# Exp in place in PSUM, low halves of the probabilities on VectorE, and scaling and rotation of latent queries and keys on GpSimd, in a two-layer hybrid encoder

## The chip, the core and the metric

The kernel runs on one core of one Trainium2 chip. Its engines are TensorE (PE in the profile: matmul, with weight loads listed apart as PEld), VectorE (DVE), ScalarE (ACT), GpSimd (POOL) and SyncE (SP, which issues the transfers here). They run side by side, each through its own queue in order, and wait for one another by semaphores. The metric is the device time of one execution in microseconds. Before the change it is 1695.26 us, the median of three runs that lie between 1694.22 and 1695.61 us.

## What is computed

Two layers over 512 tokens with 1024 channels, all in float32. Each layer has an attention part with three branches and a gated MLP with a convolution of width three:

```python
proj = rms_norm(x) @ w_in          # latent q, latent kv, rotary key, GQA q/k/v, pool, gates
# branch A, latent attention: 8 heads, 64 plain + 32 rotary dimensions
q = rms_norm((rms_norm(c_q) @ w_uq).reshape(b, s, 8, 96), qh_g)
k = rms_norm(concat(k_nope, broadcast(k_rope_raw)), kh_g)
q, k = rope on the last 32 of 96
# branch B, grouped-query attention: 8 heads of 64, 2 key/value heads, normed and rotated
# branch C: centred mean pooling minus token, with a linear map
# both attentions: softmax(q k^T / sqrt(d)) v
merged = sum(sigmoid(gate_i) * (o_i @ w_branch_i))
x = x + merged @ w_out
x = x + (silu(conv(h @ w_up)[gate]) * conv(h @ w_up)[val]) @ w_down
```

The normalisation of q and k is a multiplication by the inverse square root of a mean square, per token and head.

## The kernel before

Everything is kept with 128 partitions. Activations of the trunk lie channel by token (`XM`, eight tiles of 128 x 512); queries and keys are made token by channel, because their norm is per token, and are turned by TensorE into channel by token.

**Two halves.** TensorE multiplies in a reduced float32 format. So each operand is split: the high half is the value rounded to that format, the low half is the value minus the high half. A product is three matmuls: high by high, high by low, low by high (`mm3`). Weights come in by SyncE's transfers as `raw`, ScalarE writes the high half `wh`, and GpSimd the low half `wl = raw - wh`, two pieces ahead of their use (`w_ahead`, `w_split`).

**Order.** The whole order on all engines is written out when the kernel is built, by a small planner (`Clock`). It keeps a time for each engine, adds a price for each operation (`Engine`, with one price per element and one fixed), and emits the steps of a `chain` when their predecessor should be done. What an operation costs in the planner decides where its instruction stands in its engine's queue. At run time each queue is worked in that order, and only semaphores make it wait. `pick` and `copy` choose an engine for a low or a high half by the planner's times.

**Attention.** `attention` walks a plan for eight heads, for grouped queries first (gqa) and then for the latent branch (mla). For each head there are four `s_max` steps (scores of 128 queries by 512 keys, in PSUM tile `ps_S`, one bank; VectorE takes the negative maximum of each query, `nm`), then `m_row` (TensorE turns the maxima into a row, which VectorE places as extra rows of an operand so that they are subtracted in the matmul), then four `probs` steps: scores transposed, 128 keys by 512 queries, in `ps_ST`, two banks. For each of these tiles:

- `ex`: ScalarE takes Exp of `ps_ST` into a tile `pe` in SBUF, and the bank is free;
- `hi`: ScalarE or VectorE copies `pe` to the high half `ph`;
- `lo`: GpSimd or VectorE writes `pl = pe - ph`.

`av_hi` and `av_lo` multiply these with the high and low halves of the values into `ps_AV` (two banks); a column of ones gives the softmax sums. `o_out` copies sums and outputs, takes reciprocals on VectorE, multiplies (`oraw`), and splits the result.

Between the steps of the plan TensorE is filled with other work, the `Filler`: units of three to twelve matmuls of the gate and branch projections (`ps_acc`, two banks), and the making of the latent queries and keys. A fixed schedule by position says how many filler units are due; where the planner thinks that a step's input or bank is not ready, it lets further units go first. During the first attention, `make_q` and `make_n` produce the latent queries `MQ` and keys `MK` and the sums of their squares `ssm`. When all sums are there, one `rsqrt_steps` for queries and one for keys follow (a first guess by integer arithmetic on VectorE and three Newton steps over 32 numbers a partition), and then `q_norm` and `k_norm`: scaling by the roots, and rotation of 32 of the 96 dimensions. All this is VectorE's in the kernel before. After both attentions come the last branch, the output projection, and the MLP.

Of the kernel before, what the change touches and what calls it, by code (L numbers as in the profile page):

```python
# [42 lines left out]
P_BIAS = 1.16  # L43
C_BIAS = 0.2

PRM_AG, PRM_FG, PRM_PS, PRM_CQ, PRM_CKV = 0, 8, 16, 20, 22
# [142 lines left out]
class Engine:  # L189
# [34 lines left out]
        return self.eng.tensor_reduce(out, in_, *a, **k)  # L224

    def tensor_scalar(self, out, *a):
        self._count(out, 0.00055, 0.07)
        return self.eng.tensor_scalar(out, *a)

    def tensor_copy(self, out, in_, psum=False):  # L230
# [13 lines left out]
def trunk(ctx: ExitStack, tc: tile.TileContext, x, w, prm, gb, cst, out):  # L244
# [158 lines left out]

        return [hi, lo, add]

    def rsqrt_steps(a, n, key):

        y = small("y0", [P, 64])[:, :n]
        t = small("yt", [P, 64])[:, :n]

        def newton(to):
            V.tensor_tensor(t, y, a, ALU.mult)
            V.scalar_tensor_tensor(t, t, -0.5, y, ALU.mult, ALU.mult)
            V.scalar_tensor_tensor(to, t, 1.5, y, ALU.add, ALU.mult)
# [80 lines left out]
    def layer(l, sq, xsrc):  # L495
# [371 lines left out]
        def make_q(g):  # L867
            ws = (wnext(), wnext())
            st["la"] = LA - 1
            for b in range(4):  # L870
                if b:
                    yield
                bs = slice(b * P, b * P + P)
                acc = ps("acc")
                for kc, (wh, wl) in enumerate(ws):
                    need(("latT", l, kc))
                    lh, ll = lat[kc]
                    mm3(acc[:, :384], lh[:, bs], ll[:, bs], wh[:, :384], wl[:, :384], kc == 0, kc == 1)
                q_out(g, b, acc)
            st["la"] = LA  # L880
            if g == 1:
                chain(([("ssq", l, i, b) for i in range(2) for b in range(4)],
                       lambda: V.tensor_scalar(ss[:, 0], ss[:, 0], 1.0 / 96, EPS, ALU.mult, ALU.add)),
                      *rsqrt_steps(ss[:, 0].rearrange("p g b c -> p (g b c)"), 32, ("ssmq", l)),
                      *[z for i in range(2) for z in q_norm(i)])

        def q_out(g, b, acc):
# [15 lines left out]
        def q_norm(g):  # L903
# [4 lines left out]

            def scale(p):
                bs = slice(2 * p, 2 * p + 2)  # L910
                V.tensor_tensor(q[:, bs], q[:, bs], bc(ss[:, 0, g, bs].unsqueeze(3), [P, 2, 4, 96]), ALU.mult)

            def part(o, i):
                V.tensor_tensor(r2[:, :, :, o:o + 16], qr[:, :, :, i:i + 16], bc(sn[:, :, :, o:o + 16], [P, 4, 4, 16]),
                                ALU.mult)

            return [lambda: scale(0), lambda: scale(1), lambda: part(0, 16), lambda: part(16, 0),
                    lambda: V.tensor_tensor(qr, qr, bc(cs, [P, 4, 4, 32]), ALU.mult),
                    lambda: V.tensor_tensor(qr, qr, r2, ALU.add), lambda: done("mq", l, g)]

        def make_n(g):
            wh, wl = wnext()
# [13 lines left out]
            def sums():  # L936
                V.tensor_reduce(kss, kj_, AX.X, ALU.add)
                for i in range(2):
# [1 line left out]
                V.tensor_scalar(ss[:, 1], ss[:, 1], 1.0 / 96, EPS, ALU.mult, ALU.add)  # L940

            chain(lambda: V.tensor_tensor(kj_, krt, krt, ALU.mult), ([("ssn", l, i, p) for i in range(2) for p in range(2)], sums),
                  *rsqrt_steps(ss[:, 1].rearrange("p g b c -> p (g b c)"), 32, ("ssm", l)),
                  *[z for i in range(2) for z in k_norm(i)])
            chain(*rope_steps(krr, krt, tabm[:, 256:384].rearrange("p (b f) -> p b f", b=4),
                              tabm[:, 384:512].rearrange("p (b f) -> p b f", b=4), [P, 4, 32], 16, V),
# [24 lines left out]
        def k_norm(g):  # L971
            k = MK[g]

            def nope(p):
                bs = slice(2 * p, 2 * p + 2)
                V.tensor_tensor(k[:, bs, :, 0:64], k[:, bs, :, 0:64], bc(ss[:, 1, g, bs].unsqueeze(3), [P, 2, 4, 64]),
                                ALU.mult)

            def rope():
                V.tensor_tensor(k[:, :, :, 64:96], bc(krr[:, :, None, :], [P, 4, 4, 32]),  # L980
                                bc(ss[:, 1, g].unsqueeze(3), [P, 4, 4, 32]), ALU.mult)

            return [([("krr", l)], rope), lambda: nope(0), lambda: nope(1), lambda: done("mk", l, g)]
# [37 lines left out]
        def attention(kind, fill, okey, odst):  # L1021
# [106 lines left out]
            def probs(h, k):  # L1128
# [58 lines left out]
            def o_out(h):  # L1187
# [340 lines left out]
```

## Time and profile before

The profiled execution took 1693.48 us; from its first to its last instruction are 1691.7 us, at a mean granted TensorE clock of 0.995.

| engine | busy us | share of the span | instructions |
|---|---|---|---|
| TensorE, matmul | 1649.7 | 98% | 7360 |
| TensorE, weight load | 1336.5 | 79% | 7360 |
| VectorE | 946.2 | 56% | 1520 |
| ScalarE | 775.4 | 46% | 1361 |
| GpSimd | 962.6 | 57% | 759 |

The first layer's two attentions lie between about 120 and 370 us, the second layer's between about 955 and 1205 us. The probabilities are 128 tiles: 128 Exp operations on ScalarE, 102 high halves there and 26 on VectorE, 109 low halves on GpSimd and 19 on VectorE.

A row of a group gives the line of the kernel and the engine, the operation, output and inputs with their shapes, the count, the busy time and the mean in ns of one, and then the idle time in front of them with what ended it. Lines 209, 216, 220 and 224 are those of the planner's helpers, so the tile names tell which step a row is. In a row of the timeline the first two numbers are start and duration in us, and the bracket is the idle time of that engine just before. A row of windows has the stretch, its length, busy time and count for PE, PEld, DVE, ACT and POOL, the granted clock, the share of the transfer engines, and GB/s.

### The profile page before, as it was taken

How to read it: one execution, taken by the hardware profiler on the slowest of the kernel's cores; microseconds unless marked ns; L12 is line 12 of the kernel's file. 1: busy time of each engine (PE TensorE's matmuls, PEld its weight loads, DVE VectorE, ACT ScalarE, POOL GpSimd, SP SyncE). 2: the span in 40 equal slices, each digit the busy share in tenths (PEclk: the TensorE clock that was granted, in tenths of full speed). 3: DMA queues.
4: the chain of work that ended last, by engine and by line, in shares of the span. 5: the costliest groups of instructions: out<-in, count | busy, mean ns of one | idle time of the engine just before them, and what ended most of it. 6: DMA issues, size and time to landing. Idle time of an engine off the chain costs nothing.

```text
span 1691.7 us, 20364 instructions
## 1 busy us (share of the span) xinstructions
PE 1649.7 (98%) x7360; PEld 1336.5 (79%) x7360; DVE 946.2 (56%) x1520; ACT 775.4 (46%) x1361; POOL 962.6 (57%) x759
## 2 busy tenths in 40 slices
PE   8989989999999999999999998999999999999999
PEld 7777667778888888888887786777888888888887
DVE  7776966643357666630157769666433666667100
ACT  5357645653344444432334575456434444444221
POOL 4435645764566656655544466556645665666543
PEclk9999999999999999999999999999999999999999
DMA  4221111113323232333332211111233222222331
GB/s 172 91 72 57 56 48 50 38 63 112 125 88 96 92 100 90 98 109 116 100 106 79 81 44 57 62 38 38 81 115 116 88 100 99 88 97 90 112 119 56
DMA packets 44596, 145.40 MB, mean 86 GB/s; under 512 B 5072, under 2 KB 6352, under 8 KB 44496
## 3 DMA queue, kind: packets, MB, share of 16 engines
q1 hardware_dynamic: 44352, 144.10, 25.7%
q8 instruction: 58, 0.95, 0.2%
q14 instruction: 42, 0.34, 0.1%
q10 hardware_dynamic: 144, 0.01, 0.0%
HBM read 139.90 MB, written 4.19 MB: 85 GB/s over the span
## 4 chain that ended last, share of the span: by engine, by line
PE 89%; DVE 6%; issue 2%; ACT 1%; POOL 1%; DMA 1%; SPq 0%; POOLq 0%; ACTq 0%; DVEq 0%
PE ps_acc L341 40%; PE ps_ST L341 23%; PE ps_AV L341 22%; PE ps_S L341 2%; PE ps_mi L345 1%; PE ps_mi L341 1%; DVE MQ L216 1%; POOL wl L216 1%; DVE yt L220 1%; DVE rp L216 1%; DVE nm L224 1%; DVE osum L236 0%; DVE ssm L224 0%; DVE tabg L216 0%; DMA raw<-w 0%
## 5 line engine op out<-in xcount | busy, mean ns | idle before, releaser
L216 POOL TENSOR_TENSOR wl<-raw,wh 128x512 fp32r<-128x512 f32 (+1 forms) x514 | 680.4, 1333 | 493.5 <-ACT wh L209 437.1
L209 ACT ACTIVATE wh<-raw 128x512 fp32r<-128x512 f32 (+3 forms) x522 | 313.7, 607 | 189.7 <-PE ps_ST L341 87.8
L220 DVE SCALAR_TENSOR_TENSOR a<-u,prm,a 128x512 f32<-128x512 f32 x176 | 242.3, 1377 | 79.8 <-ACT a L209 74.2
L341 PE MATMUL ps_acc<-HH,wh 128*128 128x512 f32 x592 | 236.2, 399 | 5.0 <-DVE XM L220 4.4
L341 PE MATMUL ps_acc<-HH,wl 128*128 128x512 f32 x592 | 234.9, 397 | 0.0
L341 PE MATMUL ps_acc<-HL,wh 128*128 128x512 f32 x592 | 234.9, 397 | 0.0
L216 POOL TENSOR_TENSOR pl<-pe,ph 128x512 fp32r<-128x512 f32 x109 | 143.1, 1313 | 114.2 <-ACT ph L209 77.9
L341 PEld LDWEIGHTS ps_acc<-HH,wh 128*128 128x128 f32 x592 | 112.5, 190 | 33.2 <-ACT wh L209 4.9
L341 PEld LDWEIGHTS ps_acc<-HH,wl 128*128 128x128 f32 x592 | 112.3, 190 | 26.3
L341 PEld LDWEIGHTS ps_acc<-HL,wh 128*128 128x128 f32 x592 | 112.5, 190 | 25.4
L209 ACT ACTIVATE pe<-ps_ST 128x512 f32<-128x512 f32 x128 | 76.1, 594 | 115.9 <-PE ps_ST L341 114.4
L224 DVE TENSOR_REDUCE nm<-ps_S 128x1 fp32r<-128x512 f32 x128 | 87.8, 686 | 55.5 <-PE ps_S L341 55.2
L341 PE MATMUL ps_AV<-HH,wh 128*128 128x512 f32 x288 | 113.8, 395 | 0.0
L341 PE MATMUL ps_AV<-HH,wl 128*128 128x512 f32 x288 | 113.7, 395 | 0.0
L341 PE MATMUL ps_AV<-HL,wh 128*128 128x512 f32 x288 | 113.7, 395 | 0.0
L216 POOL TENSOR_TENSOR al<-a,ah 128x512 fp32r<-128x512 f32 x44 | 58.1, 1321 | 84.8 <-ACT ah L209 58.5
L341 PE MATMUL ps_ST<-HH,wh 128*128 128x512 f32 x240 | 94.9, 395 | 0.0
L341 PE MATMUL ps_ST<-HH,wl 128*128 128x512 f32 x240 | 94.8, 395 | 0.0
L341 PE MATMUL ps_ST<-HL,wh 128*128 128x512 f32 x240 | 94.7, 395 | 0.0
L209 ACT ACTIVATE a<-u,prm 128x512 f32<-128x512 f32 x88 | 71.7, 815 | 27.6 <-DVE u L216 27.3
L209 ACT ACTIVATE ah<-a 128x512 fp32r<-128x512 f32 x44 | 27.8, 631 | 117.5 <-DVE u L240 112.0
L209 ACT ACTIVATE a<-a 128x512 f32<-128x512 f32 x44 | 27.8, 632 | 115.4 <-DVE u L240 115.4
(339 smaller groups left out, 3551.2 us busy)
## 6 DMA issues: line engine op xcount, KB each, us to landing
raw<-w SPq DMA_DIRECT2D x228, 512.0 KB, 3.4
raw<-w SPq DMA_DIRECT2D x13, 384.0 KB, 2.9
XM<-x SPq DMA_DIRECT2D x16, 256.0 KB, 3.8
raw<-w SPq DMA_DIRECT2D x6, 448.0 KB, 3.3
xsp<-XM SPq DMA_DIRECT2D x8, 256.0 KB, 2.0
XM<-xsp SPq DMA_DIRECT2D x8, 256.0 KB, 3.1
out<-XM SPq DMA_DIRECT2D x8, 256.0 KB, 2.4
raw<-w SPq DMA_DIRECT2D x4, 432.0 KB, 3.0
```

The source lines that it names most:

```text
L209: return self.eng.activation(out, in_, func, **k)
L216: return self.eng.tensor_tensor(out, *a)
L220: return self.eng.scalar_tensor_tensor(out, *a)
L224: return self.eng.tensor_reduce(out, in_, *a, **k)
L341: PE.matmul(o, lhsT=lhsT, rhs=rhs, start=start, stop=stop)
L345: PE.transpose(o, src, ident)
```

## The change

Five things are edited. Exp now writes back into its PSUM bank, and there is no `pe` tile. The high half is copied out of PSUM, priced as such in `copy`. The low half is always VectorE's, taken from PSUM, and the bank is free only after it. The Newton steps of the latent queries' and keys' roots, their scalings, and the rotation of the queries are GpSimd's; there a Newton step is four instructions instead of three. The multiplication of an output by its reciprocal sums is GpSimd's but for the last pair of heads. The planner gets a price for `tensor_scalar` on GpSimd; its other prices and the plan's numbers stay.

```diff
     def tensor_scalar(self, out, *a):
-        self._count(out, 0.00055, 0.07)
+        self._count(out, *((0.0043, 0.2) if self.kind == "Pool" else (0.00055, 0.07)))
...
-    def rsqrt_steps(a, n, key):
+    def rsqrt_steps(a, n, key, eng=None):
...
         def newton(to):
+            if eng:
+                eng.tensor_tensor(t, y, a, ALU.mult)
+                eng.tensor_tensor(t, t, y, ALU.mult)
+                eng.tensor_scalar(t, t, -0.5, 1.5, ALU.mult, ALU.add)
+                eng.tensor_tensor(to, t, y, ALU.mult)
+                return
             V.tensor_tensor(t, y, a, ALU.mult)
...
-                      *rsqrt_steps(ss[:, 0].rearrange("p g b c -> p (g b c)"), 32, ("ssmq", l)),
+                      *rsqrt_steps(ss[:, 0].rearrange("p g b c -> p (g b c)"), 32, ("ssmq", l), G),
...
             def scale(p):
                 bs = slice(2 * p, 2 * p + 2)
-                V.tensor_tensor(q[:, bs], q[:, bs], bc(ss[:, 0, g, bs].unsqueeze(3), [P, 2, 4, 96]), ALU.mult)
+                G.tensor_tensor(q[:, bs], q[:, bs], bc(ss[:, 0, g, bs].unsqueeze(3), [P, 2, 4, 96]), ALU.mult)
...
-                    lambda: V.tensor_tensor(qr, qr, bc(cs, [P, 4, 4, 32]), ALU.mult),
-                    lambda: V.tensor_tensor(qr, qr, r2, ALU.add), lambda: done("mq", l, g)]
+                    lambda: G.tensor_tensor(qr, qr, bc(cs, [P, 4, 4, 32]), ALU.mult),
+                    lambda: G.tensor_tensor(qr, qr, r2, ALU.add), lambda: done("mq", l, g)]
...
-                  *rsqrt_steps(ss[:, 1].rearrange("p g b c -> p (g b c)"), 32, ("ssm", l)),
+                  *rsqrt_steps(ss[:, 1].rearrange("p g b c -> p (g b c)"), 32, ("ssm", l), G),
...
-                pe, ph, pl = slot("pe"), slot("ph", F32R), slot("pl", F32R)
+                ph, pl = slot("ph", F32R), slot("pl", F32R)
...
                 def ex():
-                    A.activation(pe[:, :T], sc, AF.Exp)
-                    free("ST")
+                    A.activation(sc, sc, AF.Exp)
 
                 def hi():
-                    copy(ph[:, :T], pe[:, :T], False)
+                    copy(ph[:, :T], sc)
                     done(*key("ph", h, k))
 
                 def lo():
-                    pick(P_BIAS).tensor_tensor(pl[:, :T], pe[:, :T], f(ph[:, :T]), ALU.subtract)
+                    V.tensor_tensor(pl[:, :T], sc, f(ph[:, :T]), ALU.subtract)
+                    free("ST")
                     done(*key("pl", h, k))
...
-                    steps += [lambda: V.tensor_tensor(raw[:, :T], raw[:, :T], sums[:, :T], ALU.mult),
+                    steps += [lambda: (V if h == 7 else G).tensor_tensor(raw[:, :T], raw[:, :T], sums[:, :T], ALU.mult),
```

The two rotation products of the queries (`part`) and the scalings of the keys (`nope`, `rope`) change their engine from `V` to `G` in the same way.

More of the change, by code (lines that the diff above doesn't have):

```diff
@@ L42 @@
 W_BIAS = 2.54
-P_BIAS = 1.16
 C_BIAS = 0.2
@@ L910, in scale @@
                 bs = slice(2 * p, 2 * p + 2)
-                V.tensor_tensor(q[:, bs], q[:, bs], bc(ss[:, 0, g, bs].unsqueeze(3), [P, 2, 4, 96]), ALU.mult)
+                G.tensor_tensor(q[:, bs], q[:, bs], bc(ss[:, 0, g, bs].unsqueeze(3), [P, 2, 4, 96]), ALU.mult)
             def part(o, i):
-                V.tensor_tensor(r2[:, :, :, o:o + 16], qr[:, :, :, i:i + 16], bc(sn[:, :, :, o:o + 16], [P, 4, 4, 16]),
+                G.tensor_tensor(r2[:, :, :, o:o + 16], qr[:, :, :, i:i + 16], bc(sn[:, :, :, o:o + 16], [P, 4, 4, 16]),
                                 ALU.mult)
             return [lambda: scale(0), lambda: scale(1), lambda: part(0, 16), lambda: part(16, 0),
-                    lambda: V.tensor_tensor(qr, qr, bc(cs, [P, 4, 4, 32]), ALU.mult),
-                    lambda: V.tensor_tensor(qr, qr, r2, ALU.add), lambda: done("mq", l, g)]
+                    lambda: G.tensor_tensor(qr, qr, bc(cs, [P, 4, 4, 32]), ALU.mult),
+                    lambda: G.tensor_tensor(qr, qr, r2, ALU.add), lambda: done("mq", l, g)]
         def make_n(g):
@@ L975, in nope @@
                 bs = slice(2 * p, 2 * p + 2)
-                V.tensor_tensor(k[:, bs, :, 0:64], k[:, bs, :, 0:64], bc(ss[:, 1, g, bs].unsqueeze(3), [P, 2, 4, 64]),
+                G.tensor_tensor(k[:, bs, :, 0:64], k[:, bs, :, 0:64], bc(ss[:, 1, g, bs].unsqueeze(3), [P, 2, 4, 64]),
                                 ALU.mult)
             def rope():
-                V.tensor_tensor(k[:, :, :, 64:96], bc(krr[:, :, None, :], [P, 4, 4, 32]),
+                G.tensor_tensor(k[:, :, :, 64:96], bc(krr[:, :, None, :], [P, 4, 4, 32]),
                                 bc(ss[:, 1, g].unsqueeze(3), [P, 4, 4, 32]), ALU.mult)
```

## The prediction

> **What bounds the kernel now.** I read the head of the page first, then the busy time by 40 us windows, then TensorE's waits, and last the timeline around each wait.
>
> ```profile
> span 1691.7 us, 20364 instructions
> PE 1649.7 (98%) x7360; PEld 1336.5 (79%) x7360; DVE 946.2 (56%) x1520; ACT 775.4 (46%) x1361; POOL 962.6 (57%) x759
> ```
> ```profile
> 200.00:240.00 40.00, 34.93 (x149) 26.71 (x148) 31.42 (x53) 22.81 (x41) 22.24 (x18) 0.91 0.13 40
> 320.00:360.00 40.00, 40.00 (x182) 31.70 (x181) 25.13 (x37) 22.43 (x41) 27.82 (x23) 1.00 0.12 40
> ```
> ```profile
> 774.69 15.30 PE ps_acc L341 x66
> ```
>
> TensorE is the bound: 42.0 us (1691.7 − 1649.7) of its span are idle, and a full-width matmul issues every 15.30/66 = 0.232 us (row of the chain of waits). The change leaves the count and shapes of the matmuls alone, so it can win only idle time and lost clock, and lose by making new idle time. The second attention of a layer (320 to 360 us) has none to win; the end of the first (200 to 240 us) lacks 5 us, and its granted clock is 0.91. In the waits view (total, times, longest):
>
> ```profile
> PE ps_S L341 <- DVE nm L224: 13.0, 5, 4.2
> ```
> The same waits in the timeline, the bracket being the idle time before the row:
> ```profile
> 180.13 0.50 PE L341 MATMUL ps_S<-ka,qa 128*128 128x512 f32 x1 [1.98 <-DVE nm L224]
> 185.56 0.50 PE L341 MATMUL ps_S<-ka,qa 128*128 128x512 f32 x1 [0.73 <-DVE nm L224]
> 188.17 0.22 PE L341 MATMUL ps_mi<-idr,nm 128*4 128x128 f32 x1 [0.26 <-DVE nm L224]
> 211.13 0.50 PE L341 MATMUL ps_ST<-qb,kb 68*128 68x512 f32 x1 [0.55 <-DVE qb L216]
> 218.62 0.80 PE L341 MATMUL ps_S<-ka,qa 128*128 128x512 f32 x1 [4.22 <-DVE nm L224]
> ...
> 1018.18 0.50 PE L341 MATMUL ps_S<-ka,qa 128*128 128x512 f32 x1 [1.94 <-DVE nm L224]
> 1048.83 0.50 PE L341 MATMUL ps_ST<-qb,kb 68*128 68x512 f32 x1 [0.52 <-DVE qb L216]
> 1056.30 0.56 PE L341 MATMUL ps_S<-ka,qa 128*128 128x512 f32 x1 [4.17 <-DVE nm L224]
> ```
> There is one bank for the scores whose maximum is sought, so the next such matmul waits until the reduction `nm` has read the last. What kept `nm` is on VectorE's timeline:
> ```profile
> 177.04 1.22 DVE L220 SCALAR_TENSOR_TENSOR yt<-yt,y 128x32 f32<-128x32 f32 x1
> 178.30 1.18 DVE L220 SCALAR_TENSOR_TENSOR ssm<-yt,y 128x32 f32<-128x32 f32 x1
> 179.41 0.68 DVE L224 TENSOR_REDUCE nm<-ps_S 128x1 fp32r<-128x512 f32 x1
> ...
> 213.06 2.73 POOL L216 TENSOR_TENSOR pl<-pe,ph 128x512 fp32r<-128x512 f32 x2 [2.99 <-ACT ph L209]
> 214.67 1.17 DVE L216 TENSOR_TENSOR yt<-y,ssm 128x32 f32<-128x32 f32 x1
> 215.87 1.19 DVE L220 SCALAR_TENSOR_TENSOR yt<-yt,y 128x32 f32<-128x32 f32 x1
> 217.88 0.68 DVE L224 TENSOR_REDUCE nm<-ps_S 128x1 fp32r<-128x512 f32 x1
> ```
> The inverse square root of the latent queries and keys stands ahead of `nm`, and steps of 32 elements last 1.2 us while POOL is inside a low half (213.06 to 215.79). The Trainium skill, "SBUF — State Buffer", Who interferes with whom, gives the cause as a port pair that GpSimd shares with a VectorE operation reading two SBUF inputs; the rows agree. The clock after these stalls:
> ```profile
> 218.00:222.00 4.00, 3.38 (x8) 2.71 (x9) 3.57 (x6) 1.54 (x3) 0.30 (x1) 0.50 0.00 0
> 222.00:226.00 4.00, 4.00 (x15) 3.10 (x15) 2.25 (x4) 0.00 (x0) 1.69 (x2) 0.78 0.31 84
> ...
> 1018.00:1022.00 4.00, 3.82 (x11) 3.01 (x12) 3.92 (x6) 1.51 (x3) 1.64 (x3) 0.63 0.41 131
> 1056.00:1060.00 4.00, 3.71 (x9) 2.97 (x10) 3.24 (x6) 1.54 (x3) 0.86 (x1) 0.57 0.29 112
> ```
> Busy time times (1 − clock) is what the lower clock costs: 1.69 + 0.88 + 1.41 + 1.60 = 5.6 us.
>
> **The change, part by part.**
>
> *Inverse square roots, scaling and rotation to POOL.* On VectorE the chain in front of `nm` goes. If nothing else comes late, the eight waits go: 7.74 us in the first layer, 6.63 in the second, 14.4 in all, and the 5.6 us of clock with them: −20.0 us.
>
> What is late next is the rest of the key sum. These rows stay on VectorE:
> ```profile
> 208.71 1.45 DVE L216 TENSOR_TENSOR rp<-krt,tabm 128x64 f32<-128x64 f32 x2
> 211.31 0.68 DVE L224 TENSOR_REDUCE ssm<-mns 128x8 f32<-128x512 f32 x1
> ```
> In the new order there stand between the second and third `nm` of the last query head two lows (0.69 each), the reduction (0.68), and the key's square, products and one add (about 2.4 by the rows from 208.12 to 210.36): 4.5 us. The TensorE work from that head's second score matmul to its fourth is 5.2 us by widths; the reductions need 1.2 + 4.5 + 0.7 = 6.4. So 1.2 us of wait remain, and some 0.3 at the transposition of the maxima behind them: 1.5 us a layer, +3.0. Nothing is the lower bound, the old 4.2 a layer the upper.
>
> POOL loses its 109 lows and gains the moved work:
> ```profile
> L216 POOL TENSOR_TENSOR pl<-pe,ph 128x512 fp32r<-128x512 f32 x109 | 143.1, 1313 | 114.2 <-ACT ph L209 77.9 <-DVE ph L232 20.5 <-PE ps_ST L341 9.9
> L216 POOL TENSOR_TENSOR wl<-raw,wh 128x512 fp32r<-128x512 f32 x474 | 644.4, 1369 | 443.9 <-ACT wh L209 387.9 <-PE ps_acc L341 32.1 <-PE ps_AV L341 13.2
> L216 POOL TENSOR_TENSOR wl<-raw,wh 128x256 fp32r<-128x256 f32 x8 | 6.0, 744 | 0.8 <-ACT wh L209 0.8
> 256.01 1.29 POOL L216 TENSOR_TENSOR wl<-raw,wh 128x512 fp32r<-128x512 f32 x1 [0.23 <-POOL kh L240]
> ```
> From 256 to 512 elements POOL takes (1369 − 744)/256 = 2.4 ns an element over 0.12 us. No POOL row shows 32 elements or these broadcasts, so the prices are estimates from those rows: 768 elements 2.0 us, 512 1.37, 256 0.74, 32 elements 0.2, and 0.23 more where a step waits for the step before it on POOL (last row), as each of the twelve of a root does: 0.43, so 5.2 us a root; bounds 0.2 (no hop) and 0.8 (twice). A layer's query chain is 5.2 + 4 × 2.0 + 4 × 0.74 + 4 × 1.37 = 21.6 us, the key chain 5.2 + 6 × 1.37 = 13.4, and six multiplications of outputs by reciprocals, also moved, 8.2: 86 us over both layers against 143 that leave. POOL has the room. The queue order matters: the low weight halves `wl` stand behind these steps. The tightest is the first half of the gate weights behind the twelve steps and two 768-element scalings, 9.2 us. By widths it is needed 18 us after the last query product is issued; the product, its copy, square and sum, and two weight halves queued ahead take some 6.5 of them, and its own subtraction 1.37: about 1 us to spare. The other weights behind the chains have 2 us or more. I take +1.0 in both layers together; bounds 0 and, at 1.6 times the prices (14.7 for 9.2), 4.5 us a layer (9). The scaled keys have cover:
> ```profile
> 223.90 0.68 DVE L216 TENSOR_TENSOR MK<-MK,ssm 128x512 f32<-128x512 f32 x1
> ```
> ```profile
> L345 PE MATMUL ps_mi<-C,MK x64: 270/272/276, 254.5 to 1179.7; 128*96 128x128 f32 x64
> ```
> They are done near 225 us and first turned at 254.5, 30 us later, more than the 13.4 us of the chain; the queries are ready still earlier. The moved output products wait for no one near: the branch matmuls that use them come after the attention, and the last pair stays on VectorE.
>
> *Low halves on VectorE, out of PSUM.*
> ```profile
> L216 DVE TENSOR_TENSOR pl<-pe,ph 128x512 fp32r<-128x512 f32 x19 | 16.8, 889 | 5.6 <-ACT ph L209 5.5
> L216 DVE TENSOR_TENSOR gt<-ps_acc,rbc 128x512 f32<-128x512 f32 x44 | 30.4, 690 | 58.6 <-PE ps_acc L341 58.2
> L216 DVE TENSOR_TENSOR MQ<-MQ,ssm 128x768 f32<-128x768 f32 x8 | 9.5, 1192 | 0.1
> ```
> All 128 lows are on VectorE in the new order. With one operand in PSUM I price them by the product `gt`, 0.69 us, not by the 0.89 of lows with both in SBUF: 88 us, less 17 that were there. What leaves VectorE (scalings, as `MQ<-MQ,ssm`, rotations, roots, twelve output products) is some 58 us, so it gains about 15 net. In the first attention the lows about replace the burst near 175 to 215 us; in the second VectorE goes from 25.13/40 = 63% to about four fifths busy.
>
> *Exp in place.* A bank is now held until its low is read. The pieces:
> ```profile
> L209 ACT ACTIVATE pe<-ps_ST 128x512 f32<-128x512 f32 x128 | 76.1, 594 | 115.9 <-PE ps_ST L341 114.4
> L209 ACT ACTIVATE ph<-pe 128x512 fp32r<-128x512 f32 x102 | 64.4, 631 | 4.2
> L209 ACT ACTIVATE kh<-ps_mi 96x512 fp32r<-96x512 f32 x14 | 8.3, 590 | 0.0
> ...
> L341 PE MATMUL ps_AV<-pl,vmh 128*128 128x512 f32 x64 | 25.3, 395 | 0.0
> ```
> No ACT row writes PSUM. The nearest rows read it and write SBUF, so I take 0.59 for Exp, as before, with 0.4 and 0.8 as bounds. The hold after the last issue is 0.16 (395 − 232) + 0.59 + 0.59 (the high, priced by `kh` out of PSUM) + 0.69 + four hops of 0.04 = 2.2 us; before it was 0.8. There are two banks. Over the 32 score groups of a first attention, TensorE's own work between the end of one and the next use of its bank is never under 3.0 us in the new order, so nothing waits unless VectorE is late by 0.8. The `pe` tiles go and free slots of the shared pool; no row shows TensorE waiting for a slot, so I count nothing. VectorE often has one operation ahead (0.69), seldom two: +1.0 a layer, +2.0; bounds 0 and 5 a layer.
>
> *The end of the second attention.* The planner counts a bank as busy for longer and spends its filler units early. In the old order each last score group and product has a filler triple between; in the new one the last head runs bare: four score triples alternate with value triples. From the end of a score triple to its low's matmul lie 8 × 0.232 = 1.86 us (three times) and 5 × 0.232 = 1.16 (the last), against 2.2 needed: 3 × 0.34 + 1.04 = 2.1 us a layer, +4.2. With Exp at 0.4 it would be 3 × 0.15 + 0.85 = 1.3 a layer, with it at 0.8 and VectorE busy (0.69 each time) some 5. The Trainium skill, "ScalarE: Activation LUTs", Step-by-step: what each stage is for, holds ScalarE's way to PSUM for faster than its way to SBUF; no run yet shows it, and by it the end would cost about 2.6 in both layers in place of 4.2. The final filler, 312 matmuls for 318, needs no result of that head for 11 us.
>
> The sum: −20.0 + 3.0 + 1.0 + 2.0 + 4.2 = −9.8 us. The profiled run took 1693.48 us, 0.1% under the median of 1695.26; its 1691.7 us span is the part that moves. So 1683.7 in that run, 1685.5 as a median.
>
> **The rivals.**
>
> *Everything fits.* The key sum, lows and weights cost nothing, and only the bare end stays, at 2: 1695.3 − 20.0 + 2 = 1677. For it: the second attention runs today without a wait. Against: the key sum's count.
>
> *The wait only changes its cause.* `nm` waits behind lows instead of roots, at the upper bounds of the first two VectorE costs: −20.0 + 8.4 + 1.0 + 10 + 4.2 = +3.6 at the extreme, about −3 midway between it and the sum: 1692. For it: VectorE's business in the second attention. Against: lows with a PSUM operand should not stretch to 1.2 us.
>
> *POOL too slow (slower).* If the short steps and the broadcast scalings cost 1.6 times my price or more, the gate weights come late by 4.5 us a layer behind the query chain, again by about as much behind the key chain and the output products, and each gap over 2 us brings about 1.5 us of lower clock, as above: 2 × (4.5 + 4.5 + 3) = 24 in place of 1.0, so −10.8 + 24 = +13: 1708. The sign turns at about 1.35 times. For it: chained tiny steps, unpriced. Against: 57 us less work on POOL.
>
> **How the numbers follow.** Change as summed 0.45, everything fits 0.22, cause changes 0.15, POOL too slow 0.18. A difference under 0.2% (3.4 us) can't be told from none. The first two are faster; the third is mostly the same, faster in a fifth; the fourth is slower in four fifths. Faster 0.71, same 0.13, slower 0.16. The range 1674 to 1699 leaves out the worst of the POOL case and little below; the likeliest case alone is 1680 to 1690.
>
> **What would show it.** Right: no `ps_S` wait on `nm` over 2 us, granted clock 1.00 from 200 to 240 us, lows at 0.69, and waits of a few tenths at the bare end of the second attention. Wrong: `ps_acc` waiting for POOL's `wl` just behind the roots, root steps of POOL beyond 0.7 us, or many short `ps_ST` waits on VectorE's `pl`.

## The result, and the profile after

The changed kernel takes 1685.81 us (median of four runs, 1685.66 to 1686.38) against 1695.37 us (1694.22 to 1695.61) of the kernel before on the same chip: a ratio of 0.995, with a 95% interval of 0.9938 to 0.9962. The profiled execution has a span of 1684.1 us (1691.7 before). In all that follows, run labels such as e1 are kernels of the experiments below.

The head of the page of the changed kernel:

```profile
span 1684.1 us, 20306 instructions
PE 1649.9 (98%) x7360; PEld 1332.9 (79%) x7360; DVE 952.3 (57%) x1542; ACT 773.0 (46%) x1364; POOL 885.1 (53%) x746
```

TensorE does the same 1649.9 us of work, and its idle time falls from 42.0 to 34.2 us. VectorE is busy 6 us longer, POOL 77.5 us less. The same two windows of 40 us as in the prediction (busy time of each engine, then granted clock, DMA share, GB/s), and the one behind them:

```profile
200.00:240.00 40.00, 39.10 (x182) 30.98 (x181) 29.72 (x53) 26.13 (x47) 29.35 (x39) 1.00 0.21 63
...
320.00:360.00 40.00, 39.40 (x177) 30.39 (x175) 28.63 (x43) 21.15 (x38) 18.97 (x17) 1.00 0.13 40
360.00:400.00 40.00, 38.99 (x164) 30.13 (x164) 16.34 (x23) 17.93 (x32) 16.48 (x14) 1.00 0.29 93
```

The end of the first attention went from 34.93 to 39.10 us of work in 40, and from a clock of 0.91 to 1.00. The end of the second attention, full before (40.00 from 320 us on, and from 360 us on the row below of the kernel before), now has idle time.

```profile
360.00:400.00 40.00, 40.00 (x174) 32.15 (x173) 13.56 (x19) 17.59 (x31) 23.68 (x19) 1.00 0.31 95
```

TensorE's waits, changed kernel (total, times, longest, us), without the lines that stand within 0.1 us of before and one that fell (`ps_acc` behind VectorE's `wl`, 1.6 for 2.7):

```profile
PE ps_acc L340 <- ACT mns L208: 3.0, 2, 1.5
PE ps_AV L340 <- ACT ph L208: 2.6, 6, 0.6
...
PE ps_acc L340 <- POOL wl L215: 1.2, 2, 0.6
...
PE ps_ST L340 <- DVE qa L215: 0.6, 2, 0.3
PE ps_mi L340 <- DVE nm L223: 0.5, 1, 0.5
...
PE ps_S L340 <- DVE nm L223: 0.2, 1, 0.2
```

The 13.0 us of `ps_S` behind `nm` are down to 0.2, and 0.5 at the transposition of the maxima. New are 3.0 us behind the squares of the latent keys (`mns`), 2.6 behind high halves and 0.6 behind `qa` at the bare end, and 1.2 behind POOL's `wl`.

For a sum by stages I took the time from the first to the last matmul of a stage and subtracted what its matmuls need by their widths (0.232 us for 512 columns, 0.175 for 384, 0.135 for 256, 0.09 for 128, as undisturbed rows follow each other). What is left is lost time: waits, lower clock, the slower restart after a wait (the row behind it lasts 0.50 us in place of 0.40), and a small rest. Some matmul records are missing, so a figure is good to about 1 us. The lost times are those of the one profiled run of each kernel, the times are medians; for e3m (profiled 1692.3) and f2 (1686.5) the two lie apart. Lost us, first and second layer:

| kernel | first attention | second attention, middle | second attention, end | time, us | ratio to before, 95% |
|---|---|---|---|---|---|
| before | 13.3, 11.3 | 2.0, 2.0 | 0.2, 0.2 | 1695.4 | 1 |
| changed | 4.0, 3.9 | 1.9, 2.1 | 3.5, 3.5 | 1685.8 | 0.9938 to 0.9962 |
| e1 | 3.4, 3.4 | 1.7, 1.9 | 0.1, 0.2 | 1676.2 | 0.9877 to 0.9910 |
| e2 | 9.6, 15.7 | 1.8, 1.9 | 6.3, 7.5 | 1709.6 | 1.0076 to 1.0106 |
| e8 | 5.6, 5.2 | 1.7, 2.0 | 3.5, 3.5 | 1687.8 | 0.9946 to 0.9976 |
| e4 | 4.5, 3.8 | 2.0, 1.8 | 3.5, 3.5 | 1684.3 | 0.9927 to 0.9957 |
| e3m | 4.6, 4.0 | 8.0, 8.1 | 1.4, 1.4 | 1690.6 | 0.9967 to 0.9986 |
| e10 | 5.0, 5.1 | 1.8, 1.7 | 3.6, 3.6 | 1687.7 | 0.9943 to 0.9972 |
| p3 | 4.2, 3.0 | 1.8, 1.9 | 3.5, 3.5 | 1684.6 | 0.9925 to 0.9958 |
| p8 | 9.1, 9.3 | 1.9, 2.1 | 3.5, 3.5 | 1706.4 | 1.0052 to 1.0082 |
| f1 | 2.2, 7.3 | 1.0, 1.4 | 0.2, 0.2 | 1676.2 | 0.9873 to 0.9903 |
| f2 | 7.0, 5.9 | 3.0, 2.8 | 0.2, 0.2 | 1689.6 | 0.9954 to 0.9990 |
| f3 | 10.5, 11.4 | 1.8, 2.1 | 0.2, 0.2 | 1692.9 | 0.9982 to 1.0001 |
| f4 | 2.8, 3.5 | 2.1, 2.0 | 0.2, 0.2 | 1676.5 | 0.9875 to 0.9905 |

From the kernel before to the changed one that is −16.7 us in the first attentions and +6.6 at the ends of the second ones, −10.1 together, against −9.6 by the medians. The experiments ran on chips where the kernel before took 1693.96 us (e1, e2, e8, e4), 1694.90 (e3m, e10, p3, p8) and 1694.83 (f1 to f4); where a run is compared with the changed kernel, I put that at 0.995 of these, 1685.5 to 1686.4.

### The profile page after: what moved, and what is told of

Read it like the earlier page. It is cut to its first block, busy times and chain, and to the rows that moved or that the text cites. A ratio compares the mean times of both kernels' runs of the same rounds, so it can differ in the third digit from the quotient of the medians.

```text
span 1684.1 us, 20306 instructions
## 1 busy us (share of the span) xinstructions
PE 1649.9 (98%) x7360; PEld 1332.9 (79%) x7360; DVE 952.3 (57%) x1542; ACT 773.0 (46%) x1364; POOL 885.1 (53%) x746
## 4 chain that ended last, share of the span: by engine, by line
PE 88%; issue 5%; DVE 2%; ACT 2%; POOL 2%; DMA 1%; SPq 0%; POOLq 0%; ACTq 0%; DVEq 0%
PE ps_acc L340 40%; PE ps_ST L340 22%; PE ps_AV L340 22%; PE ps_S L340 2%; POOL wl L215 2%; PE ps_mi L344 1%; PE ps_mi L340 1%; ACT ps_ST L208 0%; DVE tabg L215 0%; ACT ph L208 0%; DMA raw<-w 0%; DMA prm<-prm 0%; DVE wl L215 0%; ACT qa L208 0%; ACT wh L208 0%
## 5 line engine op out<-in xcount | busy, mean ns | idle before, releaser
L208 ACT ACTIVATE ps_ST<-ps_ST 128x512 f32<-128x512 f32 x128 | 74.5, 582 | 121.6 <-PE ps_ST L340 121.2
L215 DVE TENSOR_TENSOR pl<-ps_ST,ph 128x512 fp32r<-128x512 f32 x128 | 87.1, 681 | 27.6 <-ACT ph L208 27.0
```

Of the source, the lines that this page charges most:

```text
L208: return self.eng.activation(out, in_, func, **k)
L215: return self.eng.tensor_tensor(out, *a)
```

## The experiments

**e1: only the normalisation of latent queries and keys to POOL.** The first part of the change alone; Exp, halves and output products as before.

```diff
-                    *rsqrt_steps(ss[:, 0]..., 32, ("ssmq", l)),
+                    *rsqrt_steps(ss[:, 0]..., 32, ("ssmq", l), G),
...
-                V.tensor_tensor(q[:, bs], q[:, bs], bc(ss[:, 0, g, bs]...), ALU.mult)
+                G.tensor_tensor(q[:, bs], q[:, bs], bc(ss[:, 0, g, bs]...), ALU.mult)
...
```

> The old kernel with one part of the change alone: the inverse square roots, the scalings and the rotations go to POOL; Exp, high and low halves and the output products stay as they were, so 87 of 128 low halves are still POOL's, and the end of the second attention keeps its filler triples. Theory A (the gain is the roots leaving the queue ahead of nm, and the bare end is what the change loses): the waits on nm of over 1 us and the lower clock from 200 to 240 us go (-14 to -20 us), no wait appears in the last 10 us of the second attention: 1676 to 1682 us, under the changed kernel's 1685.8. Rival B (the roots can go to POOL only because the low halves leave it; with both, POOL is late): TensorE waits for POOL's wl or pl in the first attention, 1688 to 1696 us.

1676.24 us (1674.81 to 1678.04), 17.7 under the kernel before and 9 under the changed one: theory A. The first attention loses what it loses in the changed kernel, and the ends of the second attentions nothing. One wait on `nm` is left in each layer; the timeline of e1 there, with what VectorE did ahead of it:

```profile
209.68 2.56 DVE L216 TENSOR_TENSOR rp<-krt,tabm 128x64 f32<-128x64 f32 x2
...
214.50 0.22 PE L341 MATMUL ps_mi<-idr,nm 128*4 128x128 f32 x1 [1.15 <-DVE nm L224]
```

This is the key sum of the prediction: two products of 64 elements that last 1.28 us each, and 1.15 us of wait, at the transposition of the maxima.

**e2: only Exp in place and the low halves on VectorE.**

```diff
-                    A.activation(pe[:, :T], sc, AF.Exp)
-                    free("ST")
+                    A.activation(sc, sc, AF.Exp)
...
-                    pick(P_BIAS).tensor_tensor(pl[:, :T], pe[:, :T], f(ph[:, :T]), ALU.subtract)
+                    V.tensor_tensor(pl[:, :T], sc, f(ph[:, :T]), ALU.subtract)
+                    free("ST")
```

> The old kernel with the other part alone: Exp in place in PSUM and all low halves on VectorE; roots, scalings and rotations stay on VectorE too. Theory A (the queue ahead of nm is what the first attention waits for, however long a step lasts): the roots still stand ahead of nm, now with every low half beside them; at least half of the 13 us of waits remains and the bare end of the second attention (2 to 3.5 us a layer) is added: 1692 to 1702 us. Rival B (the steps of 32 elements were slow, 1.2 us, only because POOL was at its low halves): with no low half on POOL each takes some 0.3 us, nm comes in time, and the time is 1683 to 1688 us with no root on POOL at all.

1709.64 us, 15.7 slower than the kernel before and above the range of theory A. Rival B is half right, and it doesn't help. On VectorE's timeline in e2 the steps of the key root are indeed short with POOL idle beside them, yet `nm` still comes late:

```profile
215.47 0.19 DVE L220 SCALAR_TENSOR_TENSOR ssm<-yt,y 128x32 f32<-128x32 f32 x1
...
220.71 0.69 DVE L216 TENSOR_TENSOR MK<-MK,ssm 128x512 f32<-128x512 f32 x1
...
222.52 0.68 DVE L224 TENSOR_REDUCE nm<-ps_S 128x1 fp32r<-128x512 f32 x1
```

The queue in front of `nm` is now made of scalings and low halves: VectorE is busy 37.40 of the 40 us from 200 on, and TensorE's waits on `nm` in the first attentions are still 8.7 us, of 13.3 in the kernel before. So theory A has the first attentions right: by the table they lose 25.3 us in both layers, where the kernel before loses 24.6. Most of the 15.7 us are lost elsewhere, at the ends of the second attentions: 13.8 for 0.4, about twice what theory A allowed for the bare end. There too `nm` is late on a full VectorE (3.5 us in both layers), and the granted clock falls to 0.57 behind it (366 to 370 us).

Alone, the two parts give −17.7 and +15.7, which sums to −2.0; the changed kernel has −9.6, 7.6 us better. The output products, which the changed kernel moves too, are in neither part. Neither part alone tells what the whole does.

**e8: the roots back on VectorE.** The changed kernel without `G` in the two calls of `rsqrt_steps`.

> The changed kernel with only the two roots a layer (10 steps of 32 elements each) back on VectorE; scalings and rotations stay on POOL, Exp in place and low halves as in the changed kernel. Theory A (the steps themselves ahead of nm cost the time): waits on nm come back, 1.5 to 4 us a layer, 1688 to 1694 us. Rival B (the steps are short once POOL has no low halves; what mattered was the slow steps): within 1.5 us of the changed kernel's 1685.8.

1687.76 us, a ratio of 0.9946 to 0.9976: 2.3 us more than the changed kernel's 1685.5, which the intervals don't quite tell apart. The time lies between both theories; the waits are as theory A has them, for those on `nm` come back, 4.6 us in both layers in place of 0.7. TensorE's rows, first layer:

```profile
178.37 0.22 PE L340 MATMUL ps_mi<-idr,nm 128*4 128x128 f32 x1 [1.82 <-DVE nm L223]
...
214.31 0.50 PE L340 MATMUL ps_S<-ka,qa 128*128 128x512 f32 x1 [1.35 <-DVE nm L223]
```

Against the changed kernel the first attention loses 1.6 and 1.3 us more. Once no low half is on POOL, a root on VectorE lasts some 2 us (nine steps from start to start of 0.23), and by the medians moving it is worth about 2 us, a small part of the gain.

**f3: the roots alone on POOL.** The kernel before with `G` in these two calls, nothing else.

> The old kernel with the roots alone on POOL; scalings, rotations, Exp, halves and products as before. Theory A (nine steps of 1.2 us ahead of nm are the main part of the wait): most of the 17.7 us that e1 gained comes with the roots: 1677 to 1683 us. Rival B (the scalings and rotations that follow in VectorE's queue hold nm as long): waits on nm of over 1 us stay behind the scalings, 1685 to 1693 us.

1692.91 us, 0.9982 to 1.0001: no difference that could be told, so rival B. What holds `nm` is the next thing in VectorE's queue. Its timeline in f3, and TensorE's row:

```profile
220.76 1.74 DVE L216 TENSOR_TENSOR MK<-krr,ssm 128x512 f32<-128x512 f32 x1 [3.12 <-POOL ssm L216]
222.43 0.68 DVE L224 TENSOR_REDUCE nm<-ps_S 128x1 fp32r<-128x512 f32 x1
...
223.16 0.22 PE L341 MATMUL ps_mi<-idr,nm 128*4 128x128 f32 x1 [2.07 <-DVE nm L224]
```

VectorE stands 3.12 us at the scaling, which waits for POOL's root, and `nm` behind it, ready long before, waits with it. So it is the move of root and scalings together that frees `nm` (e1).

**f2: the whole change of placement.** e1, and the output products on POOL as well, as the change has it.

> The run e1 with the output products on POOL too, so the whole change of placement without Exp in place and without the low halves on VectorE. Theory A (VectorE's load in the attentions decides, POOL has room): like e1 or up to 3 us under it, 1673 to 1677 us. Rival B (POOL, with the products and 89 low halves, now runs into its limit): TensorE waits for POOL's wl or pl by more than 2 us a layer, 1679 to 1690 us.

1689.59 us, 5.2 under its kernel before where e1 was 17.7 under its own: nearer to rival B, but not by its mechanism, for no wait on POOL's `wl` or `pl` grew. Its ten runs fall apart into five of 1685.0 to 1686.7 us and five of 1692.4 to 1697.6, so the size is uncertain; even the five shorter ones, of which the profiled run is one, lie some 8 us or more above e1. In f2 VectorE's small steps lie beside a POOL that never pauses (from 199.5 to 213.4 us its rows follow each other without a gap). VectorE's timeline there, and TensorE's row:

```profile
208.92 2.02 DVE L216 TENSOR_TENSOR rp<-krt,tabm 128x64 f32<-128x64 f32 x2
210.87 1.38 DVE L216 TENSOR_TENSOR krr<-krt,tabm 128x128 f32<-128x128 f32 x1
212.28 1.27 DVE L216 TENSOR_TENSOR krr<-krr,rp 128x128 f32<-128x128 f32 x1
...
214.80 0.27 PE L341 MATMUL ps_mi<-idr,nm 128*4 128x128 f32 x1 [3.25 <-DVE nm L224]
```

In the changed kernel, without low halves on POOL, the same three take 0.35, 0.28 and 0.27 us (rows below). So moving the output products costs some 8 us or more where low halves stay on POOL. That the products as such cause it, and not the order that the planner then chose, isn't shown.

**f4: the key's own square and products on POOL.** e1 with `G` for `kj` and the two products `rp`.

> The run e1 with the rotation products and the square of the key's own 32 columns on POOL too (three small steps and their place in the queue: in e1 the two products of 64 elements took 2.56 us on VectorE beside POOL, and TensorE waited 1.15 us for nm behind them, in each layer). Theory A (that pair is the rest of the key sum's wait): the waits on nm of 2.3 us fall under 0.5, and the time by 1.5 to 3 us under e1's: 1673 to 1675 us. Rival B (POOL brings them late, the sum of the key stands and nm with it): nm waits as long or longer, 1676 to 1681 us.

1676.48 us, like e1's 1676.24; neither theory. The waits on `nm` are gone, as theory A said, but another stands in their place, 1.0 and 1.2 us in the two layers:

```profile
215.09 0.50 PE L341 MATMUL ps_ST<-qb,kb 68*128 68x512 f32 x1 [1.02 <-DVE qb L216]
```

**e4: the copy of the latent keys always on ACT.** The one new wait that the prediction didn't have is that of the bank `acc` for the squares `mns`, 1.51 us in each layer.

```diff
-                copy(MK[g][:, bs, :, 0:64], acc.rearrange(...))
+                A.activation(MK[g][:, bs, :, 0:64], acc.rearrange(...), AF.Copy)
```

> The changed kernel with the copy of the latent keys out of PSUM always on ACT, where the planner had put one of them on VectorE. Theory A (the 1.51 us that TensorE waits for its accumulation bank at 193 and 1027 us come from that copy standing behind VectorE's reciprocals, with the squares on ACT behind it): these two waits go and the time falls by 2 to 3 us, to 1683 us. Rival B (the bank is held by ACT's own queue, weights and queries ahead of the squares): the wait stays at 1 us or more, and the time within 1 us of the changed kernel's 1685.8.

1684.27 us, 0.9927 to 0.9957, not to be told from the changed kernel (1685.5 on this chip); `mns` waits of 2.8 us in all in place of 3.0: by the waits, rival B. TensorE's waits on `XM`, ahead of the attentions and untouched by the edit, are 2.5 us shorter in the profiled run (1.8 for 4.3), more than the 1.2 us by which the time is lower. ACT's queue in e4 and TensorE's row:

```profile
190.52 0.58 ACT L208 ACTIVATE MK<-ps_acc 128x512 f32<-128x512 f32 x1
190.99 0.62 ACT L208 ACTIVATE wh<-raw 128x512 fp32r<-128x512 f32 x1
191.51 0.58 ACT L208 ACTIVATE mns<-ps_acc 128x512 f32<-128x512 f32 x1
...
192.15 0.39 PE L340 MATMUL ps_acc<-wh,cth 128*128 128x256 f32 x1 [1.23 <-ACT mns L208]
```

The squares stand behind the copy and a weight half on a queue without gaps. Why that queue is fuller here than in e1, which has no such wait, stays open. Neither Exp in place nor the low halves are needed for it: f3, which has neither, waits 3.8 us for `mns`, and e10, which has all low halves on VectorE, not at all.

**e3m: fillers kept for the end.** The changed kernel with no allowance for fillers ahead of their turn in the second attention.

```diff
-                while fill.done < target + SLACK and waiting(fn, *args) and fill.step():
+                while fill.done < target + (SLACK if gqa else 0) and waiting(fn, *args) and fill.step():
```

> The changed kernel with one constant of the planner: in the second attention no filler unit is spent ahead of its turn (the allowance SLACK is 0 there, 35 elsewhere), so filler triples are left between the last head's score and value triples; the work is the same. Theory A (the bare end costs 3.5 us a layer, TensorE standing for the last head's Exp, high and low halves): the loss of that stage falls to under 1 us a layer and the time by 5 to 7 us, to 1677 to 1680 us. Rival B (the fillers are only moved: what the end wins, score matmuls in the middle of the second attention lose at banks still held by their low halves): the time stays within 2 us of the changed kernel's 1685.

1690.55 us, 4 slower than the changed kernel, and outside both ranges. Theory A is wrong where it counts: the end loses 1.4 us a layer in place of 3.5 (it said under 1), but the middle 8.0 in place of 2.0. That the fillers are only moved, as rival B had it, is right. The waits of e3m:

```profile
PE ps_mi L340 <- DVE nm L223: 5.8, 7, 1.1
```

They are not waits for a bank held by a low half, as rival B had it; TensorE stands for `nm` on a VectorE that has all the low halves. So the fillers are needed in the middle, and in this kernel the bare end is the cheaper place to pay.

**e10: the bank given back behind Exp.** The changed kernel with Exp into an SBUF tile again; all low halves stay on VectorE.

> The changed kernel with Exp written to an SBUF tile again and the bank given back behind Exp; roots and scalings stay on POOL, and all low halves stay on VectorE, now with both operands in SBUF. Theory A (the end is bare because VectorE has all the low halves, and it costs 3.5 us a layer because the values stand behind Exp and halves, not because a bank is held): the end of the second attention loses 3 to 4 us a layer as in the changed kernel, and the time is within 3 us of 1685, the low halves costing VectorE 0.7 to 0.9 us each. Rival B (holding the bank is what costs): the loss there falls under 1 us a layer and the time to 1676 to 1680 us.

1687.74 us, 1.3 over the changed kernel's 1686.4 on this chip, and the end loses 3.6 us a layer: theory A. The order is bare at the end in this kernel too, although no bank is held. So the bare end doesn't come from the bank but goes with VectorE having all the low halves; that the planner reckons VectorE as loaded and therefore spends its fillers early is an inference. Group rows of e10, where the low half reads two SBUF operands, and of the changed kernel, where one is in PSUM:

```profile
L215 DVE TENSOR_TENSOR pl<-pe,ph 128x512 fp32r<-128x512 f32 x128 | 107.4, 840 | 22.7 <-ACT ph L208 21.2
L208 ACT ACTIVATE pe<-ps_ST 128x512 f32<-128x512 f32 x128 | 76.3, 596 | 104.2 <-PE ps_ST L340 102.6
L208 ACT ACTIVATE ph<-pe 128x512 fp32r<-128x512 f32 x106 | 66.9, 631 | 3.2
```
```profile
L215 DVE TENSOR_TENSOR pl<-ps_ST,ph 128x512 fp32r<-128x512 f32 x128 | 87.1, 681 | 27.6 <-ACT ph L208 27.0
L208 ACT ACTIVATE ps_ST<-ps_ST 128x512 f32<-128x512 f32 x128 | 74.5, 582 | 121.6 <-PE ps_ST L340 121.2
L208 ACT ACTIVATE ph<-ps_ST 128x512 fp32r<-128x512 f32 x108 | 64.5, 597 | 3.3
```

In place, each step is cheaper: 0.681 for 0.840, 0.582 for 0.596, 0.597 for 0.631 us.

**f1: Exp in place only where VectorE takes the low half.** e1 with a choice for each score group: 56 of 128 in PSUM with the low half on VectorE, 72 as before.

```diff
+                    e = at["e"] = pick(P_BIAS)
+                    src = at["p"] = sc if e is V else slot("pe")[:, :T]
+                    A.activation(src, sc, AF.Exp)
+                    if e is not V:
+                        free("ST")
...
+                    at["e"].tensor_tensor(pl[:, :T], at["p"], f(ph[:, :T]), ALU.subtract)
+                    if at["e"] is V:
+                        free("ST")
```

> The kernel with the roots, scalings and rotations on POOL alone (run e1), and Exp in place only where VectorE takes the low half (56 of 128); the other 72 low halves stay POOL's, out of SBUF, with the bank given back behind Exp. Theory A (what the changed kernel loses against e1 comes from giving VectorE all the low halves, not from Exp in PSUM): the end of the second attention loses under 1.5 us a layer, and the time is 1673 to 1679 us. Rival B (any bank held until its low half is read costs TensorE): new waits on the score banks, 1680 to 1686 us.

1676.17 us: theory A. No wait on a held bank, the ends lose 0.2 us a layer. So for 56 of the tiles holding the bank is harmless. It isn't everywhere: in e2, where VectorE is full, TensorE waits 2.1 us for banks held by `pl`. And f1 keeps the output products on VectorE as well, so it doesn't divide the 9 us against the changed kernel between the low halves and the products; the changed kernel with its products on VectorE was not run. The first layer is the best of all (2.2 us lost); the second has one wait of e1's kind left, behind products `rp` that last 1.28 us each:

```profile
1038.17 0.79 PE L341 MATMUL ps_S<-ka,qa 128*128 128x512 f32 x1 [2.96 <-DVE nm L224]
```

e1, f1 and f4 can't be told apart; each beats both kernels, by about 1.1% and 0.55%.

**p3 and p8: longer roots on POOL.** The changed kernel with three and with eight more iterations in each root: added work on POOL, TensorE's order untouched.

```diff
+            for _ in range(3 if eng else 0):
+                again()
```

> The changed kernel with three more iterations in each root on POOL, 12 more steps of 32 elements, which leave the roots as they are: by the changed kernel's rows (0.33 us from step to step) some 4.0 us more in each of the four chains, and TensorE's order is the same. Theory A (POOL has room: the query chain as measured takes 3.9 us for the root and 2.9 for two scalings where 9.2 was counted with 1 us to spare, so 3.4 us are spare): 0 to 2 us slower than the changed kernel, 1685 to 1687. Rival B (POOL is near its limit, the weights are already nearly late): TensorE waits for POOL's weights for 2 us or more a layer: 1689 to 1695 us.

> As the kernel with three more iterations, with eight more: 32 more steps, some 10.6 us more in each of the four chains. Theory A (3.4 us spare on the gate weights): TensorE stands some 7 us a layer behind the query chain and less behind the key chain, with lower clock behind that: 1698 to 1715 us, and the rows of TensorE name POOL's wl. Rival B (the room is much larger than was counted, POOL catches up by its idle time): under 4 us slower than the changed kernel, 1685 to 1689 us. This is where the sign would turn if the short steps had cost four times as much.

p3: 1684.61 us, 0.9925 to 0.9958: 4.0 us more on each chain cost nothing. p8: 1706.38 us, 20 more than the changed kernel. Theory A in both. Waits of p8, and the row behind the query chain:

```profile
PE ps_acc L340 <- POOL wl L215: 18.7, 8, 5.2
```
```profile
196.26 0.80 PE L340 MATMUL ps_acc<-HH,wl 128*128 128x512 f32 x1 [4.30 <-POOL wl L215]
```

With 10.6 us more the gate weights are late by 4.30, so the chain as it is leaves about 6.3 us; theory A had 3.4. The first attention loses 5.2 us a layer more than in the changed kernel, and the stage of the latent values behind it 5.7 (6.7 in place of 1.0): 2 × (5.2 + 5.7) = 21.8, which covers the whole difference of 20.

## Why the prediction came out right

The time, 1685.8 for 1685.5, is right, and the two large terms have the right sign and place. Several terms are off, and they cancel. By place, the sum has −14.0 us in the first attentions (−20.0 + 3.0 + 1.0 + 2.0, with the whole bank term put there) and +4.2 at the ends of the second; measured are −16.7 and +6.6. The two misses, 2.7 and 2.4 us, go opposite ways, so that the time came within 0.3 us is luck; the direction and the main mechanism are not.

*Waits and clock, −20.0 with 3.0 back for the key sum.* The eight waits are gone, the clock is 1.00 where it was 0.91, and e1, with a clock of 1.00 there too, shows that the moved steps alone do this. The 0.7 us on `nm` that are left stand at 178.1 us, behind the query sum, and at 1101.9 us in a second attention. At the key sum TensorE doesn't wait at all: it was priced at 3.0 and costs nothing, because its steps were priced from rows beside POOL's low halves (`rp` 1.45 for two), and the change itself takes these away. VectorE's timeline in the changed kernel:

```profile
212.11 0.31 DVE L215 TENSOR_TENSOR kj<-krt 128x128 f32<-128x128 f32 x1
212.35 0.35 DVE L215 TENSOR_TENSOR rp<-krt,tabm 128x64 f32<-128x64 f32 x2
212.62 0.28 DVE L215 TENSOR_TENSOR krr<-krt,tabm 128x128 f32<-128x128 f32 x1
...
214.02 0.27 DVE L215 TENSOR_TENSOR krr<-krr,rp 128x128 f32<-128x128 f32 x1
```

In e1, where POOL keeps low halves, a wait of this kind is there, with 1.15 us a layer for 1.5, all of it at the transposition. The rule of the Trainium skill, "SBUF — State Buffer", Who interferes with whom, that a VectorE operation with two SBUF inputs contends with GpSimd's reads, is borne out: 0.19 us for a step of 32 elements in e2 with POOL idle, 1.2 beside its low halves, and low halves with one operand in PSUM at 0.68.

*Missing: the squares of the latent keys,* 2 × 1.51 = 3.0 us, no term of the sum. By chance it equals the 3.0 that the key sum was charged too much. e4 excludes the copy on VectorE as the cause.

*POOL's weights, +1.0.* The rows give 1.2 (two waits of 0.62), but not at the place named: they stand at 166.5 us, 11 us ahead of the root, and at the same step in the second layer. e8 and e2, with the roots on VectorE, have the same 1.2 there, so the moved roots don't cause them, and the agreement is chance. Behind the roots nothing was late. POOL's timeline in the changed kernel shows the prices, first and last step of a root and what follows:

```profile
177.54 0.25 POOL L215 TENSOR_TENSOR yt<-y,ssm 128x32 f32<-128x32 f32 x1
...
181.13 0.26 POOL L215 TENSOR_TENSOR ssm<-yt,y 128x32 f32<-128x32 f32 x1
181.47 2.90 POOL L215 TENSOR_TENSOR MQ<-MQ,ssm 128x768 f32<-128x768 f32 x2
185.57 1.29 POOL L215 TENSOR_TENSOR wl<-raw,wh 128x512 fp32r<-128x512 f32 x1 [1.20 <-ACT wh L208]
```

A root takes 3.9 us for 5.2, a scaling of 768 elements 1.45 for 2.0, and the weights behind them wait for ACT, not for POOL. So the room is about 6 us (by p8) where the prediction counted 1; 2.4 us of the difference are the prices (6.8 for 9.2), the rest would be a deadline later than was counted. The rival "POOL too slow", with the sign to turn at 1.35 times the prices (3.2 us more), fails by its threshold: p3 adds 4.0 us at no cost. Its mechanism is real: at 10.6 us more a chain p8 is slower by 20 us, about the 23 that the rival described.

*Banks and late low halves, +2.0.* Nothing: no matmul of TensorE waits for `pl`, only weight loads at the bare end do, and the middle of the second attention loses 4.0 us over both layers, as before. VectorE was counted too full: it gained 6 us where about 15 were counted, and from 320 to 360 us it is busy 28.63 of 40, 72% and not four fifths. The low half was priced right, 0.681 for 0.69, and so were Exp (0.582 for 0.59) and the high half (0.597 for 0.59). The Trainium skill, "ScalarE: Activation LUTs", Step-by-step: what each stage is for, that ScalarE's way to PSUM is the faster one, agrees in sign, with 0.582 for 0.594; at 0.012 us it changes no wait here. The 2.6 us for both layers came from the prediction's own bound of 0.4 us for Exp, which no run shows.

*The bare end, +4.2.* It is 6.6 (3.5 less 0.2 a layer). The place and the order are as foreseen, the size is not, and one reason is wrong. (The upper case, some 5 us a layer, comes to 5.7 by its own terms.) The timeline of the changed kernel at the first two of the last head's groups, with a weight load that waits for the low half:

```profile
357.66 0.63 ACT L208 ACTIVATE oh<-oraw 128x512 fp32r<-128x512 f32 x1 [3.89 <-POOL oraw L215]
358.20 0.58 ACT L208 ACTIVATE ps_ST<-ps_ST 128x512 f32<-128x512 f32 x1
358.81 0.60 ACT L208 ACTIVATE ph<-ps_ST 128x512 fp32r<-128x512 f32 x1
...
359.46 0.50 PE L340 MATMUL ps_AV<-ph,vmh 128*128 128x512 f32 x1 [0.29 <-ACT ph L208]
...
360.18 0.19 PEld L340 LDWEIGHTS ps_AV<-pl,vmh 128*128 128x128 f32 x1 [0.48 <-DVE pl L215]
...
361.80 0.50 PE L340 MATMUL ps_AV<-ph,vmh 128*128 128x512 f32 x1 [0.41 <-ACT ph L208]
```

The prediction counted only the low half's deadline. TensorE stops earlier, at the high half, which stands behind Exp on ACT, and the first Exp stood behind `oh`, whose output product the change had moved to POOL. TensorE's waits there sum to 1.6 us a layer; the other 1.7 or so go with restarts (0.50 us for 0.40) and with the weight loads, and how they divide isn't shown. The cause given, that the planner counts the bank as busy, falls with e10: the bank is given back early there, and the end is as bare and as dear. The bare order goes with the low halves on VectorE: e1, f1 and f2, which share them, keep a filled end, f2 even with the output products on POOL, while e2, with the products on VectorE, runs bare. And e3m shows that fillers saved for the end are missed in the middle.

## What to carry to other kernels

Move a chain off a queue with everything behind it that waits for its result: the root alone gained nothing measurable (f3), the root with its scalings 17.7 us (e1). When a change has two parts, cost each with the other in place, for the rows of before were measured beside work that the other part removes. And when an engine gets all of a kind of work, look not only at its busy share but at what the planner then does with its fillers: the changed kernel gave back 9 us of the 17.7, 6.6 of them at an end that had been full.

## What the runs showed of the hardware that I had not expected

POOL multiplies by one number per token and head, repeated along 64 or 96 elements, faster than it forms low halves of weights of the same size: these group rows of the changed kernel give 1.05 us for 512 elements and 1.48 for 768, against 1.36 for `wl` with 512. A table that is repeated over the heads instead (`tabm`) gains little: 1.29 us for 512.

```profile
L215 POOL TENSOR_TENSOR wl<-raw,wh 128x512 fp32r<-128x512 f32 x474 | 642.1, 1364 | 595.4 <-ACT wh L208 493.9 <-PE ps_acc L340 35.3 <-PE ps_S L340 34.2
...
L215 POOL TENSOR_TENSOR MQ<-MQ,ssm 128x768 f32<-128x768 f32 x8 | 11.6, 1478 | 0.2
L215 POOL TENSOR_TENSOR MK<-MK,ssm 128x512 f32<-128x512 f32 x8 | 8.3, 1046 | 0.0
...
L215 POOL TENSOR_TENSOR MQ<-MQ,tabm 128x512 f32<-128x512 f32 x4 | 5.2, 1293 | 0.2
```

Chained steps of 32 elements on POOL follow each other in 0.33 us, 0.08 more than they last, a third of the hop of 0.23 that I had taken from a weight half behind a copy.

In the kernel before, the length of a wait alone did not tell what the clock did after it. The wait of 1.94 us ahead of 1018.18 was followed by a granted clock of 0.63 over 4 us, the one of 1.98 us ahead of 180.13 by 1.00, as this row of its windows shows:

```profile
182.00:186.00 4.00, 3.27 (x15) 2.28 (x14) 3.97 (x4) 1.59 (x3) 3.48 (x3) 1.00 0.00 0
```
